# Attention and retention scores with 128 columns in place of 256

## The chip, the core and the metric

The kernel runs on one core of a Trainium2 chip. The metric is the time of the whole program on the device, in microseconds (us); lower is better. Engines are named as in the profile: PE multiplies matrices, PEld loads its stationary operand ahead of a product, DVE and POOL are vector engines, ACT applies functions, SP issues transfers.

## What is computed

A diffusion-style block (neighbourhood attention, a gated scan, two feed-forward parts, with modulation), then two "hybrid" layers, which the change concerns. All is float32, 512 tokens of 1024 features. A hybrid layer, cut to what matters:

```python
def dilated_window_attention(q, k, v, window, dil):      # groups: (128,1), (512,4), (2048,16), 4 heads each
    s = einsum('bcgnqd,bcgnkd->bcgnqk', qs, kk) * Dh ** -0.5
    valid = (ki >= 0) & (dist >= 0) & (dist <= span)      # a band: own block of 128 and the one before
    p = exp(where(valid, s, NEG_INF) - m);  o = p @ vv / sum(p)
# retention, 4 heads of 256:  att = (q k^T) * decay for keys not after the query;  out = att @ v
merged = sigmoid(ga) * (y_att @ w_proj_attn) + sigmoid(gr) * (y_ret @ w_proj_ret)
return x + gate * (merged @ w_out)
```

With 512 tokens, a query of the two strided groups sees only the 128 keys of its own residue class (every fourth token), and the first 128 queries of the unstrided group see only the first 128 keys. In the retention the last 128 keys are seen by the last 128 queries alone.

## The kernel before

Stages follow one another: neighbourhood attention, feed-forward, gated scan, feed-forward, then `b2` with its two hybrid layers, from about 2,120 us to the end. Every product of float32 matrices is done by `mm3` (L146 to L148): each operand is cut into a high and a low part of type float32r, and three products of parts are summed in PSUM. Weights arrive by SP's transfers as `wraw`; ACT writes the high part `whi` (L132), DVE or POOL the low part `wlo` (L135).

`b2_layer` runs over four attention heads (`b2_attend`) and then four retention heads (`b2_retain`). `dense` makes 128 features of all 512 tokens with 24 products of 512 columns into one of three PSUM tiles `pacc`; `dense_v` makes values with products of 256 columns, which for the strided groups take every fourth token as stationary operand (`x[:, t::4]`).

A head's attention has eight score tiles `s`, in this text T0 to T3 (the unstrided group, 128 queries each) and U0 to U3 (the two strided groups side by side, one residue class each). The pool has two buffers for `s`. Each tile's chain: products on PE; on DVE a reduce that adds the mask and takes the row maximum (L1442), then a multiply for the bias (L1443); on ACT the exponential with its row sum (L1447, ACTIVATE and ACTIVATION_READ_ACCUMULATOR); then the buffer is free for the tile after next. T0 has three products, as T1 to T3 have; U0 to U3 have six.

The order on each engine is made by the tile framework's scheduler from the dependencies, not by hand: products of the next head (`between()`, tiles `pacc`) are put between the score products. In this text they are called fillers. Engines execute their own queue strictly in that order.

In the retention (`b2_retain`), key tile m makes scores for the queries from m on; `f` is the width of the product, `n` of what is used.

Of the kernel before, what the change touches and what calls it, by code (L numbers as in the profile page):

```python
# [18 lines left out]
D = 1024  # L19
# [6 lines left out]
KBASE = (0, 8, 24, 32)          # first key column of each 16-column query block  # L26
BOFF = (16, 8, 8, 0)            # its offset in the wide bias table
BVAR = (0, 1, 1, 2)

# columns of the packed per-feature vectors  # L30
# [10 lines left out]
# 2 pi in parts of 8 bits, whose products with small integers are exact  # L41
# [12 lines left out]
class Acts:  # L54
    """Activations with features on the partitions, as float32r parts [hi, lo]: 512 latent tokens and,
    in smaller tiles, 256 context tokens."""
# [18 lines left out]
class Prog:  # L75
# [14 lines left out]
    # ---------------------------------------------------------------- helpers  # L90
# [8 lines left out]
    def t2(self, name="t", n=512, dt=F32):  # L99
        """a short-lived tile of up to 2 KB a partition"""  # L100
        return self.sb.tile([128, n], dt, name=name, tag="t2", bufs=6)
# [7 lines left out]
    def weights(self, srcs, kt, own=None):  # L109
        """Loads float32 columns and cuts each value into two float32r parts whose sum it is.  # L110
        Returns a function of the row block that gives the two parts."""
# [27 lines left out]
    def wcols(self, w, c0, n, k0=0, kt=KT):  # L139
        """[128, kt, n] view of columns c0.. of a [K, N] weight."""  # L140
        return w[k0 * 128:(k0 + kt) * 128, c0:c0 + n].rearrange("(k p) n -> p k n", p=128)

    def mm3(self, out, lh, rh, first, last):
        """out (+)= (lh0+lh1).T @ (rh0+rh1), the product of the low parts being below float32."""
        nc = self.nc
        nc.tensor.matmul(out, lh[0], rh[0], start=first, stop=False)  # L146
        nc.tensor.matmul(out, lh[0], rh[1], start=False, stop=False)  # L147
        self.lastmm = nc.tensor.matmul(out, lh[1], rh[0], start=False, stop=last)  # L148

    def rsqrt(self, ss, scale, n, name="rs"):  # L150
        """(ss*scale + EPS) ** -0.5 on a few columns: Newton's steps from a first guess by the exponent."""
# [11 lines left out]
    def row_rstd(self, x, room):  # L163
        """(mean of squares + EPS) ** -0.5 of the rows of a token tile, half a row at a time; room: for the squares"""
# [12 lines left out]
    def rstd(self, ss, n, d):  # L177
        """(ss / d + EPS) ** -0.5 of sums of d squares, by GpSimd"""
# [6 lines left out]
    # ---------------------------------------------------------------- constants  # L185
    def setup(self):
# [11 lines left out]
        # the gated scan's lower bounds of the forget gates, and one less them  # L198
# [6 lines left out]
        # silu of the three conditioning vectors; c and c_ctx interleaved for the first products  # L205
# [7 lines left out]
    # ---------------------------------------------------------------- modulation vectors  # L213
    def ada_first(self):
        """shift and scale of the first norm for c and c_ctx, as columns: A = g * (1 + scale), shift"""
# [68 lines left out]
def ffn(S, l, xs, xout, more):  # L284
    """xout(t) is the residual tile that gets gate * swiglu(h); the last two of six tiles are the context's"""
# [16 lines left out]
    def dense(f):  # L302
        """a and u columns of feature tile f"""
# [18 lines left out]
    for gi, gn in enumerate(groups):  # L322
        gts = []
        for f in range(f0, f0 + gn):
# [5 lines left out]
            if l == 0:      # from columns first to rows first  # L330
# [12 lines left out]
            # a gate that this layer itself waits for comes at once  # L343
# [58 lines left out]
# which 1024 columns of a modulation matrix, and the names its vectors go by  # L402
# [3 lines left out]
def gemv_jobs(S, pool, wname, layer, part, vecs, ps, tag):  # L406
    """vec @ w + b for one 1024-column part, 256 columns a step, as a row in DRAM: S.rows[part, layer, v]."""
# [35 lines left out]
def gemv_rows(S, pool, wname, layer, part, ps, tag):  # L443
    """The same for c and c_ctx on the tensor engine, where other work leaves it idle."""
# [33 lines left out]
def gemv_flush(S, pool, ps, tag, after):  # L478
    """the sums over the partitions of the steps so far, behind other products so that no engine waits for them"""
# [21 lines left out]
def gate_bcast(S, part, layer, v, pool=None, tag="gate", bufs=2):  # L501
    """a modulation row on every partition"""
# [6 lines left out]
def mod_cols(S, sh, sc, g, layer, v):  # L509
    """(g * (1 + scale), shift) as columns"""  # L510
# [10 lines left out]
def residual_add(S, x, p, gate, c0, n):  # L521
    """x[:, c0:c0+n] += gate * p"""
# [6 lines left out]
def out_product(S, w, tok, xs, gates, own, tags, after=None):  # L529
    """xs[t] += gate * (h @ w): the first half of the columns for all the token tiles at once, row block by row  # L530
    block; then the other half a token tile after the other"""
# [25 lines left out]
def norm_block(S, xs, A, sh, rows, room, banks, hold=(), both=False, split=True):  # L557
    """h = x / rms(x) * A + sh of token tiles as two parts, with features on the partitions; rows(k): where
    row block k goes; room(): space for the scaled rows of a tile; banks: tags of the PSUM tiles to turn it in"""
# [43 lines left out]
def grid_rows(ap, t):  # L603
    """rows of a [512, D] array for the token tile of grid columns 16t.., column-major"""
    return bass.AP(tensor=ap.tensor, offset=ap.offset + 16 * t * D, ap=[[D, 16], [GW * D, ROWS], [1, D]])
# [15 lines left out]
def l0_start(S):  # L621
    nc, sb, ps, I = S.nc, S.sb, S.ps, S.I
    # residual rows, column-major grid order for the latent tokens
# [20 lines left out]
def na_heads(S, na, hT, jobs):  # L644
    """Head pair after head pair. The order of the instructions is the one they are written in: three phases of
    the attention, each a step behind the one before, with the products of the next heads between them."""
# [45 lines left out]
    # the products of the first heads come before the attention  # L692
# [63 lines left out]
class Feed:  # L756
    """A sequence of products, and of what follows from them some time of products later."""
# [8 lines left out]
    def then(self, lag, fn, cost=0.0):  # L766
        """after the last product and lag"""
# [11 lines left out]
def feed_weights(S, F, src, me):  # L779
    """the parts of a weight chunk, two row blocks at a time, as soon as the last one's products let them go"""  # L780
# [140 lines left out]
def o_row(oT, pr, lat):  # L921
    """outputs of a head pair, [feature, token]"""
# [5 lines left out]
def split_rows(S, oR, oT, pr):  # L928
    """the outputs of a head pair as two parts"""
# [7 lines left out]
def na_scores(S, na, st, g, h, b, qk, mask):  # L937
    """a step of the attention: softmax of 16 columns' queries, or of 128 context tokens"""
# [24 lines left out]
def na_max(S, me, h, b):  # L963
    """minus the maxima; the scores are negative ones"""
# [62 lines left out]
# ---------------------------------------------------------------- gated scan layer  # L1027
# [3 lines left out]
def view(t, off, dims):  # L1031
    """free-dimension pattern over a tile"""
# [80 lines left out]
def hg_qg(S, hT, w, c0, tag):  # L1113
    """silu of two heads' 256 columns from c0 on"""
# [16 lines left out]
def hg_head(S, hT, w, h, V, lb, om, masks, q, reads):  # L1131
# [4 lines left out]
    # forget gates; index 0 is the backward direction in f, the forward one in K  # L1136
# [26 lines left out]
    # Q: q (1 - lb) times the decays; the keys stay without their (1 - lb)  # L1163
# [10 lines left out]
    for li, m in enumerate(LEVELS):  # L1174
# [9 lines left out]
        # decays over whole blocks join  # L1184
# [19 lines left out]
    # states between the 128-token blocks: keys with tokens on the partitions, then k.T @ v  # L1204
# [41 lines left out]
def hg_read(S, h, on, g):  # L1246
    """output of a head, normed and gated, [feature, token]"""
# [16 lines left out]
# ---------------------------------------------------------------- hybrid layers  # L1264
# [3 lines left out]
def b2_tables(S):  # L1268
    """attention masks, and cos and sin of the rotary angles, [angle, position]"""
# [52 lines left out]
def dense(S, W, H, j):  # L1322
    """features on the partitions: 128 columns of a weight chunk for all the tokens"""
# [6 lines left out]
def dense_v(S, W, H, classes=False, parts=False, rows=False):  # L1330
    """tokens on the partitions: 256 columns of a weight chunk as [token, tile, column]; classes: tile r
    holds every fourth token from r on; parts: as two parts; rows: row block by row block"""
# [28 lines left out]
def b2_layer(S, l):  # L1361
# [5 lines left out]
    # what comes between the two parts of a head's attention: the first products of what follows  # L1367
# [24 lines left out]
def b2_qk(S, H, w, h, g):  # L1392
    """queries and keys of a head in a group"""
# [4 lines left out]
    for j, name in enumerate("qk"):  # L1398
        p = dense(S, W, H, j)
        hi, lo = parts = part_tiles(S, name)  # L1400
        if g:           # every fourth token together
# [8 lines left out]
def b2_attend(S, H, w, h, V, y, first, between):  # L1410
# [8 lines left out]
    # Maxima and sums, [layout, here or in the other layout, tile, which]: a layout has 128 tokens in a row  # L1419
    # (the first group) or every fourth token (the other two) in a tile.  # L1420
# [3 lines left out]
    for lay in range(2):  # L1424
        for i in range(4):
            S.mark("b2_att")
            s = ps.tile([128, 512], F32, name="s", tag="s", bufs=2)
            if lay == 0:
                k0 = max(i - 1, 0) * 128
                S.mm3(s[:, 0:256], [x[:, i * 128:(i + 1) * 128] for x in q[0]], [x[:, k0:k0 + 256] for x in k[0]],  # L1430
                      True, True)
                n = 256 if i else 128
                s, mask = s[:, 0:n], S.bmask[:, 256 - n:256]
                pr = lambda x: x[:, 0:n]
            else:
                for g in (1, 2):
                    S.mm3(s[:, g * 256 - 256:g * 256], [x[:, i * 128:(i + 1) * 128] for x in q[g]],
                          [x[:, i // 2 * 256:i // 2 * 256 + 256] for x in k[g]], True, True)
                pr = lambda x: x.rearrange("p (g n) -> p g n", g=2)
                s, mask = pr(s)[:, :, i % 2 * 128:i % 2 * 128 + 128], pr(S.bmask[:, 256:512])  # L1440
# [8 lines left out]
    # each layout's figures in the other's order, by way of DRAM  # L1449
# [57 lines left out]
def b2_rotated(S, H, w, h, name, c0):  # L1507
    """queries or keys of a retention head, rotated"""
# [17 lines left out]
def b2_retain(S, H, w, l, h, early, before):  # L1526
    """the retention of a head and what ends it; before: what ends the head before"""
# [18 lines left out]
    # scores with keys on the partitions, for the queries from the key tile on  # L1546
    S.mark("b2_ret")
    At = []
    for m in range(4):
        n = 512 - 128 * m  # L1550
        f = max(n, 256)
# [90 lines left out]
def b2_final(S):  # L1642
    """the last norm of a token tile"""
# [38 lines left out]
def _rpb_wide(rpb):  # L1682
    """[head, (col, row), (u, key row)]: rpb[head, key row - row + 7, u - col - 1], zero where there is none"""
# [20 lines left out]
def _lv_mask():  # L1704
    """which (key, query) pairs of a 128-token block the joins of 1, 2, 4, 8 and 16 tokens hold"""
# [55 lines left out]
```

## Time and profile before

| | |
|---|---|
| three runs | 3571.23, 3572.5, 3573.5 us; median 3572.5 us |
| span of the profiled execution | 3573.2 us (the page gives no other time for it) |
| PE busy | 3460.9 us, 97% of the span |
| DVE, ACT, POOL busy | 55%, 35%, 20% |
| chain of work that ended last | PE 83%, DVE 9%, DMA 4% |
| mean granted TensorE clock | 0.990 |

"Busy" of PE is the sum of stretches in which a product's record is open, and records of successive products overlap: a product of 512 columns has a record of 0.39 us but the next one starts after 0.23 us. So the busy share hides short waits; the distance between starts tells what a product costs.

### The profile page before, as it was taken

What the parts mean: (1) busy time and instruction counts of PE and PEld (TensorE: products, weight loads), DVE (VectorE), ACT (ScalarE), POOL (GpSimd) and SP (SyncE); (2) the same over time, 40 slices, a digit from 0 to 9 for tenths busy, and PEclk for the clock granted to TensorE, in tenths of its full rate; (3) what the DMA queues carried; (4) which work ended last, traced back from release to release, by engine and by line L of the source; (5) the groups of instructions that cost most, each with busy time, mean ns of one, the idle gap of its engine ahead of it and who ended that gap; (6) DMA issues with size and microseconds to landing.
All of it is one profiled execution on the core that took longest, in us unless ns stands there. A gap on an engine that the chain in (4) does not pass through costs nothing.

```text
span 3573.2 us, 49417 instructions
## 1 busy us (share of the span) xinstructions
PE 3460.9 (97%) x18796; PEld 2928.4 (82%) x18796; DVE 1963.4 (55%) x3910; ACT 1254.8 (35%) x2472; POOL 717.7 (20%) x651
## 2 busy tenths in 40 slices
PE   7999999999999899999999999999999999999999
PEld 5988857788778788887877888988888888888887
DVE  6566655847875566577787452336542413255523
ACT  4454534222222433334323243333333433333332
POOL 2112212111111301112222221111222311112122
PEclk9999999999999999999999999999999999999999
DMA  6121153423552211112565332222223322222332
GB/s 199 45 59 49 54 165 106 131 61 106 160 151 68 60 36 60 48 48 77 167 196 174 96 97 79 66 77 72 83 87 103 130 65 77 71 72 90 91 101 98
DMA packets 444734, 336.92 MB, mean 94 GB/s; under 512 B 39968, under 2 KB 417104, under 8 KB 444496
## 3 DMA queue, kind: packets, MB, share of 16 engines
q1 hardware_dynamic: 444064, 333.36, 31.1%
q8 instruction: 147, 2.41, 0.3%
q0 software_dynamic: 432, 0.41, 0.1%
q14 instruction: 91, 0.75, 0.1%
HBM read 324.16 MB, written 8.54 MB: 93 GB/s over the span
## 4 chain that ended last, share of the span: by engine, by line
PE 83%; DVE 9%; DMA 4%; ACT 2%; issue 2%; POOL 1%; SPq 0%; DVEq 0%; ACTq 0%; POOLq 0%
PE pacc L146 15%; PE pacc L147 15%; PE pacc L148 15%; PE pau L148 3%; PE pau L146 3%; PE pau L147 3%; PE po L146 2%; PE po L148 2%; PE po L147 2%; DVE gacc L432 2%; PE po L1017 2%; PE pw L148 2%; PE pw L146 2%; PE pw L147 2%; DMA araw<-ada_w 2%
## 5 line engine op out<-in xcount | busy, mean ns | idle before, releaser
L135 POOL TENSOR_TENSOR wlo<-wraw,whi 128x512 fp32r<-128x512 f32 x388 | 524.8, 1355 | 2227.8 <-ACT whi L132 2034.7
L132 ACT ACTIVATE whi<-wraw 128x512 fp32r<-128x512 f32 x776 | 483.6, 631 | 817.2 <-PE pacc L147 354.0
L135 DVE TENSOR_TENSOR wlo<-wraw,whi 128x512 fp32r<-128x512 f32 x388 | 323.6, 835 | 627.0 <-ACT whi L132 625.2
L146 PE MATMUL pacc<-hT,whi 128*128 128x512 f32 x1344 | 534.0, 397 | 0.0
L148 PE MATMUL pacc<-hT,wlo 128*128 128x512 f32 x1344 | 533.5, 397 | 0.0
L147 PE MATMUL pacc<-hT,whi 128*128 128x512 f32 x1344 | 531.9, 396 | 0.0
L146 PE MATMUL pacc<-whi,hT 128*128 128x256 f32 x1056 | 340.0, 322 | 4.0 <-DVE h L593 2.6
L147 PE MATMUL pacc<-wlo,hT 128*128 128x256 f32 x1056 | 331.0, 314 | 0.0
L148 PE MATMUL pacc<-whi,hT 128*128 128x256 f32 x1056 | 330.0, 313 | 0.0
L148 PEld LDWEIGHTS pacc<-hT,wlo 128*128 128x128 f32 x1344 | 253.4, 189 | 56.6
L147 PEld LDWEIGHTS pacc<-hT,whi 128*128 128x128 f32 x1344 | 253.4, 189 | 55.3
L146 PEld LDWEIGHTS pacc<-hT,whi 128*128 128x128 f32 x1344 | 253.6, 189 | 53.5
L148 PE MATMUL pau<-hT,wlo 128*128 128x512 f32 x704 | 281.7, 400 | 4.2 <-DVE wlo L135 4.2
L146 PE MATMUL pau<-hT,whi 128*128 128x512 f32 x704 | 281.7, 400 | 1.9 <-ACT whi L132 1.2
L147 PE MATMUL pau<-hT,whi 128*128 128x512 f32 x704 | 280.6, 399 | 0.0
L432 DVE SCALAR_TENSOR_TENSOR gacc<-araw,cact,gacc 128x256 f32<-128x256 f32 x448 | 249.4, 557 | 31.1 <-DMA araw<-ada_w 13.8
L146 PEld LDWEIGHTS pacc<-whi,hT 128*128 128x128 f32 x1056 | 237.6, 225 | 11.9 <-issue 5.5
L147 PEld LDWEIGHTS pacc<-wlo,hT 128*128 128x128 f32 x1056 | 238.0, 225 | 1.2 <-DVE wlo L797 0.3
L148 PEld LDWEIGHTS pacc<-whi,hT 128*128 128x128 f32 x1056 | 237.8, 225 | 0.0
L146 PE MATMUL po<-whi,gh 128*128 128x512 f32 x440 | 176.9, 403 | 15.3 <-ACT gh L340 14.4
L147 PE MATMUL po<-wlo,gh 128*128 128x512 f32 x440 | 175.1, 399 | 0.0
L148 PE MATMUL po<-whi,gl 128*128 128x512 f32 x440 | 174.7, 399 | 0.0
(366 smaller groups left out, 6623.2 us busy)
## 6 DMA issues: line engine op xcount, KB each, us to landing
araw<-ada_w SPq DMA_DIRECT2D x96, 512.0 KB
wraw<-w_in SPq DMA_DIRECT2D x96, 512.0 KB
wraw<-ffn_w_in SPq DMA_DIRECT2D x176, 256.0 KB
wraw<-w_in SPq DMA_DIRECT2D x160, 256.0 KB
araw<-w_ada SPq DMA_DIRECT2D x48, 512.0 KB
wraw<-ffn_w_out SPq DMA_DIRECT2D x40, 512.0 KB
x<-x SPq DMA_DIRECT2D x24, 512.0 KB
wraw<-hg_w_in SPq DMA_DIRECT2D x24, 512.0 KB
```

What stands on the lines that cost most here:

```text
L132: nc.scalar.activation(hi, r, AF.Copy)
L135: eng.tensor_sub(lo, r, fr(hi))
L146: nc.tensor.matmul(out, lh[0], rh[0], start=first, stop=False)
L147: nc.tensor.matmul(out, lh[0], rh[1], start=False, stop=False)
L148: self.lastmm = nc.tensor.matmul(out, lh[1], rh[0], start=False, stop=last)
L432: nc.vector.scalar_tensor_tensor(acc, r, cv, acc, op0=OP.mult, op1=OP.add)
L1017: nc.tensor.matmul(po, v[:, vc:vc + 64], me["pT"][:, j, :], start=(j == 0), stop=(j == len(vv) - 1))
```

## The change

The change narrows three score products from 256 moving columns to the 128 that are used. T0 multiplies with its own 128 keys. Each strided tile multiplies with its own 128 keys, and its two groups now stand side by side in 256 adjoining columns of `s`, so that the reduce, the mask and the exponential are plain 256-column accesses instead of two pieces of 128. In the retention `f` becomes `n`, which alters the last key tile alone. Counted from the loops: 3 + 24 products for each of 8 attention heads and 6 for each of 8 retention heads (four of each in two layers), 264 in all. Comments that it also drops are left out here.

```diff
@@ b2_attend
             if lay == 0:
                 k0 = max(i - 1, 0) * 128
-                S.mm3(s[:, 0:256], [x[:, i * 128:(i + 1) * 128] for x in q[0]], [x[:, k0:k0 + 256] for x in k[0]],
+                n = 256 if i else 128
+                S.mm3(s[:, 0:n], [x[:, i * 128:(i + 1) * 128] for x in q[0]], [x[:, k0:k0 + n] for x in k[0]],
                       True, True)
-                n = 256 if i else 128
                 s, mask = s[:, 0:n], S.bmask[:, 256 - n:256]
                 pr = lambda x: x[:, 0:n]
             else:
                 for g in (1, 2):
-                    S.mm3(s[:, g * 256 - 256:g * 256], [x[:, i * 128:(i + 1) * 128] for x in q[g]],
-                          [x[:, i // 2 * 256:i // 2 * 256 + 256] for x in k[g]], True, True)
-                pr = lambda x: x.rearrange("p (g n) -> p g n", g=2)
-                s, mask = pr(s)[:, :, i % 2 * 128:i % 2 * 128 + 128], pr(S.bmask[:, 256:512])
+                    S.mm3(s[:, g * 128 - 128:g * 128], [x[:, i * 128:(i + 1) * 128] for x in q[g]],
+                          [x[:, i * 128:(i + 1) * 128] for x in k[g]], True, True)
+                s, mask = s[:, 0:256], S.bmask[:, 256:512]
+                pr = lambda x: x
@@ b2_retain
         n = 512 - 128 * m
-        f = max(n, 256)
+        f = n
```

The scheduler also places the work anew. PE's queue in the third attention head of the first hybrid layer, before, from the end of U1 (`s_23264`) to the start of U2 (`s_23275`); `pacc_23326` is a filler:

```order
L146 MATMUL s_23264<-kh_23173,qh_23144 128x256
L147 MATMUL s_23264<-kl_23174,qh_23144 128x256
L148 MATMUL s_23264<-kh_23173,ql_23145 128x256
L148 MATMUL pacc_23326<-hT_21165,wlo_23323 128x512
L146 MATMUL pacc_23326<-hT_21165,whi_23322 128x512
L147 MATMUL pacc_23326<-hT_21166,whi_23322 128x512
L146 MATMUL s_23275<-kh_22775,qh_22746 128x256
L147 MATMUL s_23275<-kl_22776,qh_22746 128x256
```

PE's queue at the same place in the changed kernel:

```order
L146 MATMUL s_23264<-kh_23173,qh_23144 128x128
L147 MATMUL s_23264<-kl_23174,qh_23144 128x128
L148 MATMUL s_23264<-kh_23173,ql_23145 128x128
L146 MATMUL s_23275<-kh_22775,qh_22746 128x128
L147 MATMUL s_23275<-kl_22776,qh_22746 128x128
```

The three fillers between U1 and U2 are gone from there; they stand behind U3. The 24 products of U0 to U3 now follow one another with nothing between them.

PE's queue in the same head around T2 (`s_23235`) and T3 (`s_23244`), before:

```order
L148 MATMUL s_23235<-kh_22694,ql_22666 128x256
L146 MATMUL pacc_23326<-hT_21165,whi_23318 128x512
L146 MATMUL s_23244<-kh_22694,qh_22665 128x256
L147 MATMUL s_23244<-kl_22695,qh_22665 128x256
L148 MATMUL s_23244<-kh_22694,ql_22666 128x256
L147 MATMUL pacc_23326<-hT_21166,whi_23318 128x512
```

PE's queue there in the changed kernel:

```order
L148 MATMUL s_23235<-kh_22694,ql_22666 128x256
L146 MATMUL s_23244<-kh_22694,qh_22665 128x256
L147 MATMUL s_23244<-kl_22695,qh_22665 128x256
L148 MATMUL s_23244<-kh_22694,ql_22666 128x256
L148 MATMUL pacc_23326<-hT_21165,wlo_23319 128x512
L146 MATMUL pacc_23326<-hT_21165,whi_23318 128x512
```

The filler between T2 and T3 is gone. In numbers, the fillers ahead of T2, between T2 and T3, ahead of U0 and between U1 and U2 were 15, 1, 4, 3 and are now 14, 0, 6, 0 in five of the eight heads. In the second head of each layer, whose fillers have 256 columns, they were 29, 1, 11, 5 and are 26, 1, 11, 0. In the very first head they were 12, 0, 6, 3 and are 12, 1, 4, 0.

DVE's queue in the same third head, before, for T2 and T3:

```order
L1442 ISA s_23235,stats_23215<-s_23235,bmask_21289 128x256
L1442 ISA stats_23215 128x1
L1443 TENSOR_SCALAR bnm_23216<-stats_23215 128x1
L1442 ISA s_23244,stats_23215<-s_23244,bmask_21289 128x256
L1442 ISA stats_23215 128x1
```

DVE's queue there in the changed kernel:

```order
L1442 ISA s_23235,stats_23215<-s_23235,bmask_21289 128x256
L1442 ISA stats_23215 128x1
L1442 ISA s_23244,stats_23215<-s_23244,bmask_21289 128x256
L1442 ISA stats_23215 128x1
L1443 TENSOR_SCALAR bnm_23216<-stats_23215 128x1 x2
```

The multiply of T2 now stands behind T3's reduce; so it stands in the second head's queue before the change already. POOL's and SP's queues are the same in both kernels.

## Rows read from the trace of the kernel before

**Rows 1.** The page: busy time by engine, and the chain that ended last.

```profile
PE 3460.9 (97%) x18796; PEld 2928.4 (82%) x18796; DVE 1963.4 (55%) x3910; ACT 1254.8 (35%) x2472; POOL 717.7 (20%) x651
...
PE 83%; DVE 9%; DMA 4%; ACT 2%; issue 2%; POOL 1%; SPq 0%; DVEq 0%; ACTq 0%; POOLq 0%
```

**Rows 2.** PEld's waits, 2190 us to the end: us in total, times, longest.

```profile
PEld s L146 <- ACT P L1447: 9.9, 24, 0.6
```

**Rows 3.** Timeline of the third head: start, length, engine, instruction, [idle before].

```profile
2360.94 0.19 PEld L146 LDWEIGHTS s<-kh,qh 128*128 128x128 f32 x1 [0.41 <-ACT P L1447]
...
2363.04 0.19 PEld L146 LDWEIGHTS s<-kh,qh 128*128 128x128 f32 x1 [0.40 <-ACT P L1447]
...
2363.73 0.28 PE L148 MATMUL s<-kh,ql 128*128 128x256 f32 x1
...
2364.16 0.43 DVE L1442 CUSTOM_DVE_ANT_0 s<-s,bmask 128x256 f32<-128x256 f32 x1 [1.13 <-PE s L148]
...
2364.57 0.39 PE L148 MATMUL pacc<-hT,wlo 128*128 128x512 f32 x1
...
2364.80 0.40 PE L146 MATMUL pacc<-hT,whi 128*128 128x512 f32 x1
...
2364.88 0.43 DVE L1442 CUSTOM_DVE_ANT_0 s<-s,bmask 128x256 f32<-128x256 f32 x1
2364.93 0.47 ACT L1447 ACTIVATE P<-s,bnm 128x256 f32<-128x256 f32 x1 [1.30 <-DVE bnm L1443]
...
2365.55 0.19 PEld L146 LDWEIGHTS s<-kh,qh 128*128 128x128 f32 x1 [0.56 <-ACT P L1447]
...
2365.66 0.19 PEld L147 LDWEIGHTS s<-kl,qh 128*128 128x128 f32 x1
2365.77 0.28 PE L147 MATMUL s<-kl,qh 128*128 128x256 f32 x1
...
2365.89 0.28 PE L148 MATMUL s<-kh,ql 128*128 128x256 f32 x1
...
2367.09 0.39 PE L148 MATMUL pacc<-hT,wlo 128*128 128x512 f32 x1
```

**Rows 4.** Timeline of values of a strided group, every fourth token stationary.

```profile
2315.03 0.40 PE L146 MATMUL pacc<-whi,hT 128*128 128x256 f32 x1
2315.13 0.33 PEld L147 LDWEIGHTS pacc<-wlo,hT 128*128 128x128 f32 x1
...
2315.27 0.40 PE L147 MATMUL pacc<-wlo,hT 128*128 128x256 f32 x1
```

**Rows 5.** Timeline of the first stage: three float32r transposes of 128 columns.

```profile
73.97 0.37 PE L906 MATMUL ptq<-idr,cat 128*128 128x128 f32 x3
74.18 0.35 PE L146 MATMUL pacc<-whi,hC 128*128 128x256 f32 x1
```

**Rows 6.** Timeline of the gated scan: four float32 products of 128 columns, eight records.

```profile
1279.80 1.15 PE L1182 MATMUL pl<-Q,KX 128*128 128x128 f32 x8
1280.69 0.49 PE L146 MATMUL pacc<-hT,whi 128*128 128x512 f32 x1
```

**Rows 7.** Timeline of the second head: loads for T2 and U0, first filler behind U3.

```profile
2254.82 0.19 PEld L146 LDWEIGHTS s<-kh,qh 128*128 128x128 f32 x1 [0.29 <-ACT P L1447]
...
2257.23 0.19 PEld L146 LDWEIGHTS s<-kh,qh 128*128 128x128 f32 x1 [0.21 <-ACT P L1447]
...
2261.27 0.28 PE L147 MATMUL pacc<-wlo,hT 128*128 128x256 f32 x1
```

**Rows 8.** Two stretches of the scan: us, busy time and records by engine, granted PEclk.

```profile
1615.53:1618.94 3.41, 1.26 (x6) 0.69 (x4) 3.27 (x11) 0.85 (x2) 0.00 (x0) 1.00 0.39 124
1618.94:1622.36 3.42, 3.10 (x11) 2.87 (x12) 3.42 (x8) 0.69 (x1) 0.00 (x0) 0.50 0.57 183
```

**Rows 9.** Timeline at half clock, feed-forward: successive products of 512 columns.

```profile
603.22 0.63 PE L148 MATMUL pau<-hT,wlo 128*128 128x512 f32 x1
603.64 0.63 PE L146 MATMUL pau<-hT,whi 128*128 128x512 f32 x1
```

## Prediction

> **What bounds the kernel now.** I read the page first. PE is busy for 97% of the span and holds 83% of the chain that ended last; no other engine passes 55% [rows 1]. So a change to the products counts only if it shortens or lengthens PE's own queue. Second, the waits in the hybrid layers, where the whole change lies. PE's weight loads wait 9.9 us there for a score buffer that the exponential still holds, 24 times, three times in each of eight attention heads [rows 2]; nothing else makes PE wait as often. So this stage has almost no slack in which a new wait could vanish: what PE waits more is added to the end, and a filler that is moved behind the scores must still be executed there. Third, one head in order of time.
>
> What is to be seen in the third head [rows 3]: successive score products of 256 columns start 0.12 us apart (2365.77, 2365.89), fillers of 512 columns 0.23 us apart (2364.57, 2364.80). After a wait PE first loads (2365.55), and the next load starts 0.11 us later (2365.66), when the first product can start. A load of 128 columns thus holds the loader for 0.11 us, nearly what a product of 256 columns takes. That loads can set the pace is shown where the stationary operand is every fourth token: a load's record is 0.33 us instead of 0.19, and the products, still of 256 columns, start 0.24 us apart instead of 0.12 [rows 4].
>
> **Part one: 264 narrower products.** They are 27 of the 36 score products in each attention head (T0 and U0 to U3) and 6 in each retention head. Every one still has its own load of 128 stationary columns. No row shows such a product with 128 moving columns and an ordinary load. Bounds from the nearest rows: float32r transposes of 128 columns follow one another after (74.18 - 73.97) / 3 = 0.07 us [rows 5], which would be a gain of 0.05 us each; plain float32 products of 128 columns cost 0.89 / 4 = 0.22 us each [rows 6], a loss of 0.10 us. I take 0.108 us, the pace of the loads [rows 3], because these products have the same kind of load as the 256-column products and not that of a transpose. A product then gains 0.01 us, all 264 together under 3 us, and most of that lies in tiles that wait anyhow.
>
> **Part two: the fillers.** U0 to U3 stand in one row of 24 products and share two buffers, so U2 must wait until U0's exponential is done. Take the third head, with the load for T2 (2360.94) as zero [rows 3]. Before: load for U0 at 2.10, load for U2 at 4.61, first filler behind U3 at 6.15. After:
> T2's release. DVE now reduces T3 before it multiplies for T2. That order is in the second head already, and there U0's load comes 2257.23 - 2254.82 = 2.41 after T2's [rows 7]. T2's own start is unchanged, since it waits for T0's exponential, which stands behind a table load on ACT.
> U0's last product starts at 2.41 + 6 x 0.108 = 3.06. Before, from U0's last product (2363.73) over its reduce (2364.16) and exponential (2364.93) to U2's load (2365.55) went 1.82 us [rows 3]; I take 0.05 off, because a shorter product ends sooner, and get U2's load at 4.83. U1 was finished at 3.71: PE stands still for 1.1 us where three fillers stood.
> U2's last product starts at 5.48. U1's buffer is free 0.72 us after U0's, the distance of their reduces (2364.16, 2364.88): U3's load at 5.55, its last product at 6.20, next filler at 6.31.
> That is 0.16 us later than before, and 23 - 20 = 3 fillers fewer have been executed: 3 x 0.23 = 0.69. Net loss 0.85 us a head, in five heads 4.3 us.
> The second head of each layer: before 2261.27 - 2254.82 = 6.45 [rows 7], after 6.31 by the same steps, and 8 fillers of 0.12 us are missing, 0.94: net 0.80, in two heads 1.6 us. The first head has other steps (no table load there, T2's multiply goes before T3's reduce); between nothing and 0.85 I take 0.45.
>
> **Part three: the retention.** Six products a head at 0.108 instead of 0.118: 0.06 x 8 = 0.5 us gained. The products that follow in that tile wait for earlier key tiles, so nothing new becomes late. DVE's reduces and ACT's exponentials keep their 256 elements; I cost their plainer accesses at nothing, because the number of elements stays; if they are quicker, U2's and U3's waits shrink by as much.
>
> Sum so far: 4.3 + 1.6 + 0.45 - 0.5 = 5.9 us, that is 3578.4 from the median of 3572.5. The profiled span of 3573.2 is 0.7 above the median; all steps are differences, so I add them to the median.
>
> **Part four: the clock.** In the hybrid layers PE runs at the upper of its two levels (2.4 GHz). In the scan there are falls: a stretch with 6 products and a wait of over 2 us is followed by a stretch at a granted clock of 0.50, 1.2 GHz, for 3.4 us [rows 8]. At that level fillers start 0.42 us apart instead of 0.23 [rows 3, 9], so one fall costs 3.4 x (1 - 0.23 / 0.42) = about 1.55 us. The new row of scores, 24 half-sized products and 1.1 us of standstill in 3.9 us, is thinner than anything in the hybrid layers before, though not as thin as that stretch. Whether the clock falls behind it no row decides; between none and eight falls (0 to 12 us) I take three, 4.6 us. Forecast: 5.9 + 4.6 = 10.5 us, 3583 us.
>
> **The rivals.**
> Wide cost. The 128-column float32r product is worked as slowly as a plain float32 one, 0.22 us [rows 6]. U0's last product then starts 0.66 us later, U2's load at +3.14 after U0's load, and from there U3's load waits for U1 (4.45); the next filler comes 5.98 after U0's load instead of 3.90: 2.1 us a head, and 6 x 0.11 = 0.7 in a retention head. Together 2.8 x 8 = 22 us, in all 5.9 + 22 = 28: 3600 us, without falls, since PE is then at work. For it: no ordinary 128-column float32r product is in the trace. Against it: the transposes of the same type and width at 0.07.
> Not slower: cheap products. The load hides behind the product before, and 128-column products follow at the transposes' 0.07 us [rows 5]. Six products of U0, six of U3 and six in the retention are each 0.038 shorter on the path: 0.69 x 8 = 5.5 us, which cancels the fillers' loss: 3572.9 us. It decides from a pace of about 0.07 on; slower than 0.08 the fillers win. Against it speak the load starts 0.11 us apart and the strided loads that set the pace [rows 3, 4]. Beside it stands a rule of the Trainium skill, page "TensorE: Matmul & The Clock Gate", section "Back-to-back issue gap": a sustained stream of load and product pairs at 128 columns takes about 81 ns a pair. By that figure, an estimate, the gain is 3.9 us and the sum before falls 2.0. The strided loads here, at 0.24 us for products that need 0.12, do not bear it out for this operand type.
> No fall: the forecast's fillers with a steady clock, 3576 to 3579.6.
>
> **How the numbers follow.** The forecast with one to six falls 0.52 (3580 to 3588); no fall 0.20; wide cost 0.18; cheap products 0.08; the rest 0.02. A measurement of this kernel tells some 0.2%, 7.1 us, from no change: faster is below 3565.4, slower above 3579.6. Slower: 0.52 + 0.18 = 0.70. Same: 0.20 + 0.06 = 0.26. Faster: 0.04, from cheap products at less than 0.06 us. To leave out no more than 2 in 10 the range must reach the wide cost: 3576 to 3602.
>
> **What would show it.** In the profile after: starts of the 128-column score products 0.11 us apart (0.07 or 0.22 for the rivals); one wait of PE for the exponential of about 1.1 us ahead of U2 in every head, so that rows like [rows 2] show 15 us or more instead of 9.9; 6.3 us from T2's load to the first filler behind U3; stretches at 0.50 in the slices behind 2,200 us. The prediction is wrong if the waits ahead of U2 stay near 0.4 us, or if the products' pace is not that of the loads.

## The result, and the profile after

The changed kernel takes 3592.0 us (median; 3589.8 to 3595.3) beside 3572.4 us for the kernel before: a ratio of 1.0054, with a 95% interval of 1.0039 to 1.0068, so 14 to 24 us slower. The forecast was 3583 with a range of 3576 to 3602 and 0.70 on slower. The side and the range held; the forecast was 9 us short, and 3592 lies above its case of one to six falls, which ended at 3588.

The page of the changed kernel (span; busy time by engine; the chain that ended last):

```profile
span 3588.1 us, 49419 instructions
...
PE 3468.3 (97%) x18796; PEld 2933.3 (82%) x18796; DVE 1967.8 (55%) x3910; ACT 1254.6 (35%) x2472; POOL 717.2 (20%) x651
...
PE 82%; DVE 9%; DMA 3%; ACT 2%; issue 2%; POOL 1%; SPq 0%; DVEq 0%; ACTq 0%; POOLq 0%
```

Beside [rows 1] the page tells nearly nothing: the same number of instructions on each engine and nearly the same shares. PE is busy 7.4 us *longer*, though 264 products were halved. That is a first hint of the clock, since a product at half clock has a longer record (0.63 us in [rows 9] beside 0.39 in [rows 3]). The waits tell more. PEld's waits in the changed kernel from 2190 us to the end (us in total, times, longest):

```profile
PEld s L146 <- ACT P L1447: 15.7, 23, 1.3
PEld o L146 <- DVE st L1574: 4.7, 8, 0.6
```

The first row answers to [rows 2]: 5.8 us more. The second is new. It is in the retention, and the prediction has nothing for it.

The third head of the first hybrid layer, the one that the prediction worked through (start, length, engine, instruction, idle before):

```profile
2361.35 0.19 PEld L146 LDWEIGHTS s<-kh,qh 128*128 128x128 f32 x1 [0.67 <-ACT P L1447]
...
2363.74 0.19 PEld L146 LDWEIGHTS s<-kh,qh 128*128 128x128 f32 x1 [0.35 <-ACT P L1447]
...
2364.57 0.28 PE L147 MATMUL s<-kl,qh 128*128 128x128 f32 x1
...
2364.68 0.28 PE L148 MATMUL s<-kh,ql 128*128 128x128 f32 x1
...
2365.02 0.27 PE L148 MATMUL s<-kh,ql 128*128 128x128 f32 x1
...
2366.16 0.19 PEld L146 LDWEIGHTS s<-kh,qh 128*128 128x128 f32 x1 [1.01 <-ACT P L1447]
...
2367.55 0.44 PE L148 MATMUL pacc<-hT,wlo 128*128 128x512 f32 x1
```

With T2's load (2361.35) as zero, U0's load comes at 2.39 (forecast 2.41), U2's at 4.81 (4.83) and the first filler behind U3 at 6.20 (6.31). Products of 128 columns start 0.11 us apart (2364.57, 2364.68), as the loads do. Between U1's last product (2365.02) and U2's load PE stands for over 1 us, where fillers stood in [rows 3].

To see where the time went, the table below takes the start of the first score product of each of the 16 heads of both hybrid layers (eight of attention, eight of retention) from a trace, and compares the distances from one to the next, and from the last to the end of the last vector instruction, with those of the kernel before. A positive number is time lost. The step from the last retention head of the first layer to the second layer stands apart, because merge, output and the next norm lie in it. The last columns count the separate falls of the granted clock to 0.50 within the attention heads (eight heads in each trace) and give the measured difference of the medians with its 95% interval.

| profiled kernel | 8 attention heads | 7 retention steps | step over the layer's end | sum | falls in attention heads | measured, us |
|---|---|---|---|---|---|---|
| changed, first trace | +10.6 | +4.6 | +2.0 | +17.2 | 3 | +19.6 (14 to 24) |
| changed, second trace (after2) | +18.3 | +4.7 | +1.2 | +24.2 | 6 | +19.0 (15 to 24) |
| att | +9.3 | 0.0 | +0.8 | +10.2 | 2 | +8.9 (6 to 13) |
| ret | 0.0 | +4.9 | +0.3 | +5.3 | 0 | +4.4 (1 to 7) |
| mix | -0.3 | +0.1 | +1.8 | +1.5 | 0 | 0.0 (-4 to 3) |
| pair | -5.1 | +4.4 | +2.0 | +1.3 | 0 | +1.5 (-1 to 5) |
| bn | +10.6 | +0.4 | +1.1 | +12.2 | 3 | +12.7 (9 to 18) |
| pairbn | -5.4 | +0.3 | +2.0 | -3.1 | 0 | -3.4 (-6 to 0) |
| pairw | -5.3 | +0.8 | +0.8 | -3.7 | 0 | -6.1 (-9 to -3) |
| pairw2 (pairw again) | -5.4 | +0.2 | +1.6 | -3.6 | 0 | -4.5 (-8 to -1) |
| pairU | -5.2 | +0.1 | +0.8 | -4.3 | 0 | -6.3 (-9 to -3) |
| pairT | -2.1 | -0.2 | +1.0 | -1.2 | 0 | -1.2 (-5 to 1) |

What lies ahead of the hybrid layers differs by -5.8 to +1.3 us between these traces, with one and the same program there; that is not told further. Behind the last vector instruction pair, pairbn, pairw and pairw2 take 1.0 to 1.2 us longer than the others, which is not in their sums and whose cause was not looked for.

In the changed kernel's first trace a head of attention without a fall loses 0.78 to 0.84 us (0.46 in the first head of the second layer), a step between retention heads 0.6 to 0.9 (0.3 from the last one to the end). The three attention heads with a fall lose 1.97, 2.56 and 2.43.

### The profile page after: what moved, and what is told of

The parts are those of the page before. It is cut to its first block, busy times and chain, and to the rows that moved or that the text cites. A ratio compares the mean times of both kernels' runs of the same rounds, so it can differ in the third digit from the quotient of the medians.

```text
span 3588.1 us, 49419 instructions
## 1 busy us (share of the span) xinstructions
PE 3468.3 (97%) x18796; PEld 2933.3 (82%) x18796; DVE 1967.8 (55%) x3910; ACT 1254.6 (35%) x2472; POOL 717.2 (20%) x651
## 3 DMA queue, kind: packets, MB, share of 16 engines
q8 instruction: 147, 2.41, 0.3%
## 4 chain that ended last, share of the span: by engine, by line
PE 82%; DVE 9%; DMA 3%; ACT 2%; issue 2%; POOL 1%; SPq 0%; DVEq 0%; ACTq 0%; POOLq 0%
PE pacc L146 15%; PE pacc L148 15%; PE pacc L147 15%; PE pau L148 3%; PE pau L146 3%; PE pau L147 3%; PE po L146 2%; PE po L148 2%; PE po L147 2%; DVE gacc L432 2%; PE po L1017 2%; PE pw L148 2%; PE pw L146 2%; PE pw L147 2%; DMA araw<-ada_w 2%
```

## Experiments: the two halves of the change

**Attention alone** (att) is the changed kernel with the last retention tile wide again, the diff below; **retention alone** (ret) is the kernel before with the opposite edit on the same line, and all of its attention products wide:

```diff
-        f = n
+        f = max(n, 256)
```

> Attention products narrow as in the change, the last retention tile wide again (256 columns). Theory A, read from the trace after: the loss is made of waits that lost their cover, about 0.8 us in each of eight attention heads and 0.7 us in each of eight retention heads, and of falls of the clock. By it this kernel loses the attention's 6.4 us alone over the kernel before, 3579, and up to 3584 if the three falls in attention heads come too; the wait of the retention product o for the statistics (4.7 us over 8 in the changed kernel) is gone, the wait ahead of U2 (1.1 us a head) stays. Rival, the prediction's own account: the retention edit gives 0.5 us back, so leaving it out costs 0.5 us and this kernel stays at the changed kernel's 3591 to 3592.

> Only the last retention tile narrow, all attention products wide as before. Theory A: 8 heads by 0.7 us, 3578, with the wait of o for the statistics near 4.7 us over 8, and the waits of the attention's score products as in the kernel before (9.9 us over 24). The prediction's account: 0.5 us under the kernel before, 3572, and no such wait.

Attention alone: 3583.0 beside 3574.1 us, ratio 1.0026 (1.0016 to 1.0037). Retention alone: 3578.5 beside 3574.1 us, ratio 1.0011 (1.0003 to 1.0020). PEld's waits, attention alone and then retention alone:

```profile
PEld s L146 <- ACT P L1447: 15.7, 23, 1.3
...
PEld o L1494 <- DVE PT L1489: 2.3, 8, 0.3
```

```profile
PEld s L146 <- ACT P L1447: 9.9, 24, 0.6
PEld o L146 <- DVE st L1574: 4.7, 8, 0.6
```

Each half brings its own wait and leaves the other's place alone: the o row for the statistics is missing in the first answer, and the row of [rows 2] stands unchanged at 9.9 us in the second. The prediction's account of the retention, half a microsecond won, is refuted: the edit there costs 4.4 us alone, and in ret's row of the table nearly the whole loss lies between the retention heads. The halves add to 13.3 us, less than the whole's 19.0; the intervals are wide enough for that, and the traces show that two executions of one program can differ so (falls of the clock, below). That the halves add exactly is not shown.

## Experiment: narrow products without the new order

**mix** makes only U2 and U3 narrow. By the instruction order the three fillers (five in the second head of each layer) then stay between U1 and U2, as before.

```diff
                 for g in (1, 2):
-                    S.mm3(s[:, g * 256 - 256:g * 256], [x[:, i * 128:(i + 1) * 128] for x in q[g]],
-                          [x[:, i // 2 * 256:i // 2 * 256 + 256] for x in k[g]], True, True)
+                    if i < 2:
+                        S.mm3(s[:, g * 256 - 256:g * 256], [x[:, i * 128:(i + 1) * 128] for x in q[g]],
+                              [x[:, i // 2 * 256:i // 2 * 256 + 256] for x in k[g]], True, True)
+                    else:
+                        S.mm3(s[:, g * 128 - 128:g * 128], [x[:, i * 128:(i + 1) * 128] for x in q[g]],
+                              [x[:, i * 128:(i + 1) * 128] for x in k[g]], True, True)
```

> Only U2 and U3 narrow, U0, U1, T0 and the last retention tile wide: by the instruction order the five fillers stay between U1 and U2, as in the kernel before. It asks what 12 narrow products a head cost by themselves. Theory A (the order costs, not the product): 96 products at 0.109 in place of 0.12 us give 1 us back, 3571 to 3573, no difference from the kernel before, and the wait ahead of U2 stays near 0.1 us. Rival, narrow products are dear (0.22 us each): 96 times 0.1 us more, 3582.

3574.1 beside 3574.1 us, ratio 0.9999 (0.9990 to 1.0008). Its wait row (the exponential is line 1455 there):

```profile
PEld s L146 <- ACT P L1455: 9.8, 24, 0.6
```

96 narrow products cost nothing when the fillers stay where they were, and win nothing that can be measured: the attention heads together stand 0.3 us under the kernel before. So a narrow product is neither dear (the rival of 0.22 us is refuted by this as well as by the starts 0.11 us apart) nor a gain worth counting. What costs is where the other products stand.

## Experiments: the wait of U2 taken away

Narrow strided tiles need 256 columns of a score buffer, which has 512. **pair** puts two score tiles into the halves of one buffer, and writes the products of both before their maxima and exponentials. All products are as narrow as in the change, and by the order all 24 of U0 to U3 stand in a row, as in the changed kernel, with no filler between.

```diff
-        for i in range(4):
-            s = ps.tile([128, 512], F32, name="s", tag="s", bufs=2)
+        for i0 in (0, 2):
+            bank = ps.tile([128, 512], F32, name="s", tag="s", bufs=2)
...
+            for i in (i0, i0 + 1):
+                n = 128 if lay + i == 0 else 256
+                s = bank[:, i % 2 * 256:i % 2 * 256 + n]
...
+                rows.append((i, n, s))
+            for i, n, s in rows:
...
                 nc.vector.tensor_tensor_reduce(s, s, mask, 1.0, NEG, OP.add, OP.max, mx)
...
+            for i, n, s in rows:
+                nc.scalar.activation(P[lay][i][:, 0:n], s, AF.Exp, scale=sc, bias=nm[:, lay, i:i + 1],
+                                     accum_out=X[:, lay, 0, i, 1:2])
```

> All products narrow as in the change, but two score tiles share the two halves of one 512-column bank, and both tiles' products are written before their maxima and exponentials: U2 then needs no bank that U0 or U1 still holds. By the order all 24 products of U0 to U3 stand in a row, as in the changed kernel, with no filler between. Theory A (the loss is the wait of U2 for a bank): the wait ahead of U2 is gone or under 0.2 us, the attention is back at the kernel before or 0.3 us a head under it, and with the retention's 5.6 us left the time is 3576 to 3578. Rival (24 narrow products in a row cost by themselves, by load or clock): it stays at 3590 or above.

3575.6 beside 3574.1 us, ratio 1.0004 (0.9996 to 1.0013), with the retention's loss still in it. PEld's waits:

```profile
PEld o L146 <- DVE st L1575: 4.8, 8, 0.6
PEld s L146 <- ACT P L1448: 4.6, 7, 0.7
```

The wait for the exponential falls from 15.7 us to 4.6, under the 9.9 of [rows 2]. The attention heads stand 5.1 us under the kernel before instead of 10.6 over it. The same products in the same unbroken row of 24 cost nothing once U2 has a place to write to. So the loss in the attention is the wait, and neither the width of the products nor the row of 24. In pair the fillers between the T tiles have moved too, to in front of U0, where PE now waits 0.6 us; pairU, below, leaves the T tiles as they were.

Which tiles bring the gain? **pairU** shares buffers for U0 to U3 alone (T0 to T3 and the retention as in the kernel before), **pairT** for T0 to T3 alone, with every product wide; **pairw** is pair with the wide last retention tile, and **pairw2** the same once more beside the two. The diff is that of pair, under a condition on the layout (`lay == 1` in pairU, `lay == 0` in pairT):

```diff
+            shared = lay == 1
+            if shared:
+                bank = ps.tile([128, 512], F32, name="s", tag="s", bufs=2)
```

> Shared banks in the attention, the last retention tile wide as in the kernel before. Theory A: the attention heads stand 0.5 to 0.9 us under the kernel before (as in the trace with shared banks), the retention heads level with it: 4 to 5 us under, 3569 to 3570. If the retention's loss came from the attention's narrow products and not from its own tile: 1.5 us over as with the narrow tile.

> Shared banks for U0 to U3 alone (narrow, as in the change); T0 to T3 and the retention as in the kernel before. It asks which part of the shared-bank kernel's 0.5 to 0.9 us a head comes from the strided tiles. Theory A: the 24 products gain 24 times 0.011 us, and the five fillers that stood between U1 and U2 only change places, so 0.2 to 0.4 us a head, 2 to 3 us, 3571 to 3572. Rival: the gain is in the first tiles, T2's wait for a bank, and this kernel is level with the kernel before.

> Shared banks for T0 to T3 alone, every product as wide as in the kernel before, no narrow product at all. Theory A: T2's wait (0.14 to 0.25 us a head) goes and some of U0's, 0.2 to 0.3 us a head, 2 us, 3572. Rival: the whole gain of the shared banks is here, 4 to 6 us, 3568 to 3570, and narrow products bring nothing. Or the other way: with the fillers spread as the order now has them (1, 4 and 1 between the U tiles) U1 to U3 wait and it is slower than the kernel before by up to 0.5 us a head, 3578.

> The shared-bank kernel with the wide last retention tile once more, beside its two halves on the same chip: 4 to 7 us under the kernel before, 3567 to 3570; the two halves should add to it.

pairw: 3568.2 beside 3574.3 us, ratio 0.9983 (0.9974 to 0.9992). In another set of runs, on one chip, pairU: 3569.5 beside 3575.7 us, 0.9982 (0.9974 to 0.9991); pairT: 3574.5, 0.9995 (0.9986 to 1.0004); pairw2: 3571.3, 0.9986 (0.9977 to 0.9996). The third head of pairU, from U0's load on (its exponential is line 1440):

```profile
2362.94 0.19 PEld L146 LDWEIGHTS s<-kh,qh 128*128 128x128 f32 x1 [0.40 <-ACT P L1440]
...
2364.28 0.19 PEld L146 LDWEIGHTS s<-kh,qh 128*128 128x128 f32 x1
...
2365.57 0.28 PE L148 MATMUL s<-kh,ql 128*128 128x128 f32 x1
2365.62 0.19 PEld L148 LDWEIGHTS pacc<-hT,wlo 128*128 128x128 f32 x1
2365.68 0.45 PE L148 MATMUL pacc<-hT,wlo 128*128 128x512 f32 x1
```

From U0's load to the first filler behind U3 it is 2.74 us, without a wait in between (U2's load at 2364.28 has none). In the kernel before it is 2367.09 - 2363.04 = 4.05 us, with three fillers of 0.23 in it [rows 3], so 3.36 us without them: 0.62 us gained. The table's column agrees, with 5.2 us over eight heads. Of these 0.62, the 24 products (0.112 us apart instead of 0.119) explain about 0.2; the rest is U2's wait, which the kernel before has too (0.56 in [rows 3]). Theory A's 2 to 3 us for pairU was too low because it left this wait out. pairU and pairw both beat the kernel before and the changed one, by 6 and some 25 us, and cannot be told from each other: with U2's wait gone, sharing the first tiles adds nothing that can be measured. (The 25 us are the sum of two comparisons with the kernel before; the two were not run side by side.) My rival for pairU (level with the kernel before) falls; so does the one for pairT (the whole gain). That the two halves add is not borne out by the traces: the attention heads gain 5.2 us in pairU and 2.1 in pairT, but 5.4 in pairw2. The times (6.3 and 1.2 against 4.5) are too uncertain to decide it.

## Experiments: the wait in the retention taken away

The new wait, in the first retention head of the changed kernel:

```profile
2467.97 0.99 DVE L1562 TENSOR_TENSOR Al<-a,Ah 128x384 fp32r<-128x384 f32 x2
2468.07 0.28 PE L148 MATMUL o<-V,Al 128*128 128x256 f32 x1
...
2468.88 0.28 DVE L1557 TENSOR_TENSOR a<-s,decay 128x128 f32<-128x128 f32 x1
2468.89 0.28 PE L146 MATMUL o<-V,Ah 128*128 128x256 f32 x1
2469.08 0.42 DVE L1574 BATCH_NORM_STATS2 st<-o 128x6 f32<-128x256 f32 x1
...
2469.55 0.19 PEld L146 LDWEIGHTS o<-V,Ah 128*128 128x128 f32 x1 [0.59 <-DVE st L1574]
2469.56 0.39 PE L146 MATMUL o<-V,Ah 128*128 128x256 f32 x1 [0.39 <-DVE st L1574]
```

An o tile holds the outputs of two query blocks. DVE takes the statistics of the first half (2469.08), and PE may write the second half of the tile only when that has read. The first half is complete with the product of 2468.07; the statistics come 1.01 us later, because DVE has two low parts and the decay product in its queue. The same place in the kernel before:

```profile
2466.09 0.28 PE L148 MATMUL o<-V,Al 128*128 128x256 f32 x1
...
2466.94 0.43 DVE L1574 BATCH_NORM_STATS2 st<-o 128x6 f32<-128x256 f32 x1
2467.00 0.28 PE L147 MATMUL o<-V,Ah 128*128 128x256 f32 x1
...
2467.12 0.39 PE L146 MATMUL pacc<-hT,whi 128*128 128x512 f32 x1
...
2467.35 0.28 PE L148 MATMUL o<-V,Al 128*128 128x256 f32 x1
2467.35 0.19 PEld L147 LDWEIGHTS pacc<-hT,whi 128*128 128x128 f32 x1
2467.47 0.39 PE L147 MATMUL pacc<-hT,whi 128*128 128x512 f32 x1
...
2467.70 0.28 PE L146 MATMUL o<-V,Ah 128*128 128x256 f32 x1
```

There two fillers and two more o products stand between the first half and the same product (2467.70): 1.61 us after 2466.09, while the statistics are done after 1.28. In the changed kernel these four come behind it, its turn would be at 2468.89 + 0.12 = 2469.01, and it waits until 2469.56. The statistics are done 1.43 us after the first half there, little later than before; it is the cover that went.

**bn** writes the statistics of both halves behind the products of both, in the changed kernel; **pairbn** does so in pair.

```diff
             for m in range(i + 1):
                 S.mm3(o[:, u, :], [x[:, (i - m) * 128:(i - m + 1) * 128] for x in At[m]], [x[:, m, :] for x in V],
                       m == 0, m == i)
+        for u in range(2):
             nc.vector.bn_stats(st[:, u, :], o[:, u, :])
             nc.vector.bn_aggr(mv[:, u, :], st[:, u, :])
```

> The changed kernel as it is, on the same chip as the next three. From the parts: the attention narrow alone cost 8.9 us, the last retention tile alone 4.4 us; if they add, this is 13 us over the kernel before, about 3587. From the trace after (8 attention heads by 0.8, 8 retention heads by 0.7, four falls of the clock by 1.2 to 1.7) it is 16 to 17 us, 3590.

> The change, with the statistics of the two halves of an o tile written behind both halves' products, so that no product of the second half can wait for the statistics of the first. Theory A (that wait is the retention's loss): the row of o waiting for the statistics is gone, the eight retention heads are back at the kernel before (0.7 us each), and the time is 4 to 5.6 us under the changed kernel's. Rival: the statistics were only the last of several; the product then waits as long for the parts of the scores, which come from the same VectorE queue, and nothing is won.

> All narrow, with the shared banks in the attention and the later statistics in the retention. If both repairs add: the shared-bank kernel stood 1.5 us over the kernel before with the retention's 5.6 us in it, so 3 to 5 us under the kernel before, 3569 to 3571. If the later statistics win nothing: 1.5 us over, 3575 to 3576.

The changed kernel again (after2): 3593.4 beside 3574.3 us, ratio 1.0054 (1.0041 to 1.0068). That is over both sums that were expected, 3587 and 3590; its trace has six falls of the clock in place of three. bn: 3587.0, 1.0038 (1.0025 to 1.0051), 6.3 us under after2, of which the retention's steps give 4.3 in the traces; the traces differ in falls too (three against six). pairbn: 3570.9, 0.9991 (0.9982 to 1.0000). In bn the row of o waiting for the statistics is gone, while the wait ahead of U2 stays:

```profile
PEld s L146 <- ACT P L1447: 15.7, 23, 1.3
...
PEld o L1494 <- DVE PT L1489: 2.3, 8, 0.3
```

Its seven retention steps lose 0.4 us in place of 4.7, though the tile is narrow and all its o products stand in one row. So the retention's loss was this wait. The rival, that the products would then wait for the parts of the scores, falls. pairbn has both repairs, and both show in its trace (attention -5.4, retention +0.3). A narrow last retention tile wins nothing that can be measured over the wide one (pairbn is no faster than pairw).

## The clock

Stretches of the changed kernel's first trace (us; busy time and number of records of PE, PEld, DVE, ACT and POOL; granted clock; DMA): the stretch before a fall and the fall, in the first head of the first layer, then in the third of the second layer; last the scores of the third head of the first layer, behind which there is no fall:

```profile
2204.40:2207.80 3.40, 2.54 (x23) 2.39 (x22) 1.65 (x8) 1.31 (x6) 0.00 (x0) 1.00 0.07 1
2207.80:2211.20 3.40, 3.40 (x10) 2.72 (x10) 0.93 (x6) 1.18 (x5) 0.00 (x0) 0.50 0.06 5
...
3105.50:3108.90 3.40, 2.25 (x19) 2.11 (x19) 1.83 (x9) 1.02 (x4) 0.00 (x0) 1.00 0.09 4
3108.90:3112.30 3.40, 3.40 (x9) 2.63 (x9) 1.43 (x5) 1.73 (x5) 0.00 (x0) 0.50 0.04 2
```

```profile
2363.70:2367.10 3.40, 2.53 (x21) 2.36 (x21) 1.28 (x6) 1.57 (x6) 0.00 (x0) 1.00 0.07 1
```

The same scores in pairU, without the wait:

```profile
2362.10:2365.60 3.50, 3.50 (x28) 3.03 (x26) 1.69 (x10) 1.13 (x4) 0.00 (x0) 1.00 0.07 1
```

In a fall PE gets through 9 or 10 products in 3.4 us, all of the time busy, at the lower level (0.50 of full speed, 1.2 GHz). In the attention heads, falls stand only where U2 waits for 1.0 us or more, and each of the 14 begins 0.25 to 2.1 us after U2's first product. The four profiled executions with that wait (the changed kernel twice, att, bn) have these 14 falls in 32 attention heads; the nine in which U2 waits for less than 0.6 us or not at all (kernel before, ret, mix, pair, pairbn, pairw, pairw2, pairU, pairT) have none in 72. The heads with narrow products in an unbroken row but no wait (pair, pairbn, pairw, pairw2, pairU) are among the 72. So the falls come with that wait, and the narrow products by themselves bring none. Which of the waiting heads fall is not settled: the stretch at 2363.70 reads like the one at 2204.40 and has no fall, and one program had three falls in one execution and six in another, two of these twice as long (6.8 us). That is the larger part of the difference between its two traces. One head stands out: the third of the second layer, whose U2 waits longest, fell in all four traces; the other heads fell in 10 of 28. Its wait in the first trace:

```profile
3107.29 0.19 PEld L146 LDWEIGHTS s<-kh,qh 128*128 128x128 f32 x1 [1.29 <-ACT P L1447]
```

The other heads have 1.01 there. Why this exponential came later was not looked for.

What one fall costs is told by the same head with and without it: the first head loses 1.97 us with one and 0.36 without (bn), so 1.6; the fourth of the second layer 2.43 with and 0.79 without (att), so 1.6. The third of the second layer loses 2.56; against the 0.84 of the first layer's third head that is 1.7, of which 0.3 is its longer wait, so some 1.4 for the fall. The forecast had about 1.55, worked out from [rows 3] and [rows 9].

Another fall, at the norm between the layers, is in eleven of the thirteen traces, pairT and mix among them; that step loses 0.8 to 2.0 us in them, beside 0.3 in ret, which has no such fall. It does not go with the change's waits, and nothing is concluded from it, but the sums of the traces that have it may be up to 1.7 us too high beside the one trace of the kernel before, which has none.

## Why the prediction was right or wrong

**Part one, the pace: right.** 0.108 us was taken, from the loads in [rows 3]; the trace shows 0.112, so that a product gains 0.007 us and not 0.01. The rivals at 0.07 and 0.22 are both refuted by the starts in the timeline, the second by mix as well. With the first goes, for these products, the rule of the Trainium skill (page "TensorE: Matmul & The Clock Gate", section "Back-to-back issue gap") of about 81 ns for a pair of load and product at 128 columns: here, with float32r, a pair takes 0.11 us.

**Part two, the fillers: right in mechanism and size.** The steps of the third head came within 0.02 to 0.11 us of the trace. The loss of a head was put at 0.85 and 0.80 and is 0.78 to 0.84; the first head of the first layer at 0.45, and it is 0.36 where no fall lies in it (bn). The first head of the second layer was counted at 0.85 like the rest and lost only 0.46; the third one there waited 0.3 us longer than the rest. All together some 5.9 us instead of 6.35. One reading was wrong: the first head does have a table load ahead of T0's exponential in the kernel before (1.28 us, at 2202.45 in its trace). The 0.45 taken for that head was a middle value and not worked out from it.

**Part three, the retention: wrong in sign.** The step that failed is "the products that follow in that tile wait for earlier key tiles, so nothing new becomes late". It costed the six products and did not walk along PE's queue behind them, as part two did for the attention. The new order moves two fillers and two o products there too, from in front of the second half of an o tile to behind it. They had covered DVE's statistics. In place of -0.5 us stand 4.6 us over the seven steps and some 0.3 in the last one of the first layer (ret), about 5.0 in all. This is over half of what the forecast missed. The plainer accesses, costed at nothing, did cost nothing: a reduce of 256 elements takes 0.43 us and an exponential 0.47 in the changed kernel's third head, as in [rows 3].

**Part four, the clock: right, with luck in the number.** Three falls at 1.55 us were taken, 4.6 us; the first trace has three, which cost about 4.7 us by the differences above. But six in the second trace show that three was no more than a value inside the range from none to eight. The fall between the layers, 1.7 us in this trace, was not in the forecast.

The sum of the first trace, 5.9 + 4.7 + 5.0 + 1.7, is its 17.2 us but for rounding. The forecast's 10.5 is short of it by the retention (5.5) and the fall between the layers (1.7), and 0.4 too high in the rest. The 2.4 us from there to the measured difference of the medians (19.6) lie within its interval; the traced execution is the fastest of the four (3589.8 us).

**The range: luck.** It reached to 3602 for the sake of the wide cost, which is refuted. The case that came true, fillers and one to six falls, ended at 3588, and without room made for another cause it would not have taken in the retention's 5.5 us.

## What to carry to other kernels

A smaller product changes more than its own time: where a scheduler sets the order, other work is laid elsewhere, and a wait that this work had hidden comes to light. So compare the order behind *every* edited place, however small its saving looks, and for each wait that had cover ask how long the cover still is. What a narrower result can be worth is its room: two tiles in one buffer removed a wait here that the kernel before had too (4 to 6 us faster), while the saved columns alone were worth nothing that could be measured (mix).

## What was new of the hardware

A float32r product with 128 moving columns and its own load of 128 columns starts 0.112 us after the one before, against 0.119 us with 256 moving columns (both in the score products of U0 and U1): half the columns save some 6% of the time. A standstill of some 1 us within a row of such products, in an engine that the page calls 97% busy, was followed by a stretch at 1.2 GHz in 14 of 32 heads. Where it lasted 3.4 us it cost some 1.4 to 1.6 us more, so that in the first trace the falls took nearly as much from the attention heads (4.7 us) as the waits (5.9).
